# VectorE's sums of an eighth of a gate, issued one step behind their transfer

## The chip, the cores and the metric

The kernel runs on one core of a Trainium2 chip. The metric is the device time of one execution in microseconds (us), lower is better; of several runs the median counts. A profiled execution is one more run, with every instruction recorded.

## The reference, cut to what matters

One layer of a diffusion trunk is computed for two sets of 128 tokens, a prompt and a sample, which share all weights. All numbers are float32.

```python
mod = silu(cvec) @ w_ada + b_ada                  # 2048 x 12288: six pieces of 2048 columns
sh1, sc1, g1, sh2, sc2, g2 = split(mod, 6)
h = modulate(rmsnorm(x, norm_mix_w), sh1, sc1)
hq, hi, hff, hfb, hg, cb, cc, cx, nq, nk, nv = split(h @ w_in)
o = concat(hgrn2(hq, hi, hff, hfb, hg), short_conv(cb, cc, cx), attention(nq, nk, nv))
x = x + g1 * (o @ w_out)
h = modulate(rmsnorm(x, norm_ffn_w), sh2, sc2)
x = x + g2 * ((silu(h @ w_gate) * (h @ w_up)) @ w_down)
y = rmsnorm(x, final_norm_w)
```

The two gates g1 and g2 have 2048 columns each, in four chunks of 512. Each is a product of one row (the silu of the conditioning vector, a different one for prompt and sample) with 2048 x 512 weights.

## The kernel before, in words

**Stages.** First comes the modulation of the first norm and the input projections (w_in), then from about 235 us on the feature-major input projections (w_infm), between which the HGRN scan and the attention run, then the output projection (w_out, from about 526 us), the second norm (about 626 to 647 us), gate and up (w_gate, w_up) and the down projection (w_down) in two groups. Every weight tile of 128 x 2048 is loaded by SyncE's queue into one of four buffers `raw`, split by ScalarE into a rounded part `hi` and by VectorE into a remainder `lo` (line 254, or 295 for feature-major tiles), and multiplied three times by TensorE (lines 262 and 304).

**The later modulation.** The columns of w_ada that are needed later are computed beside these stages by two queues of steps. `LATER_T` goes to TensorE: `later_pe` loads a tile and issues four small products (`ada`, line 328), each into another 32 rows of one PSUM tile. `LATER_V` holds the seven gate chunks 8, 9, 10, 11, 21, 22 and 23 and goes to VectorE: `later_dve` handles an eighth of a chunk per step. A step takes one of two buffers `araw`, writes two of its columns by a GpSimd copy from the newest activations (line 407, so that the load can't start too early), issues a 512 KB load on GpSimd's queue (line 408), and adds the eighth to the accumulator `aacc` by four VectorE instructions (line 411), one for each of two rows of weights and two sets of tokens. With the first eighth the single accumulator is cleared and the bias loaded into it (lines 400 to 404); behind the last one `later_gate` is started, which broadcasts the sum over all partitions.

**What sets the order.** The main loops call `behind(phase)` after each weight tile; `ada_step` then adds the phase's pace to each queue's credit, and a step is run for each 4.0/n of credit, where n is the number of steps of a chunk. `gate(c)` runs what is left of a chunk when its gate is needed. What the program calls in this way is no final order: a list scheduler, which goes by the order of the calls as priorities, by data dependences, by free buffers and by its own simulated times, sets the order of each engine's instructions. On the chip each engine then works through its own list in that fixed order, and waits where the next instruction isn't ready.

Of the kernel before, what the change touches and what calls it, by code (L numbers as in the profile page):

```python
# [15 lines left out]
ALU = mybir.AluOpType  # L16
# [3 lines left out]
P = 128  # L20
D = 2048
CH = 512
# [8 lines left out]
LATER_T = [12, 16, 13, 17, 14, 18, 15, 19]  # L31
LATER_V = [8, 9, 10, 11, 21, 22, 23]
# [60 lines left out]
def trunk(ctx: ExitStack, tc: tile.TileContext, a: dict):  # L93
    nc = tc.nc
# [5 lines left out]
    def sb(shape, tag, bufs, dt=F32):  # L100
        uid[0] += 1
        return pool.tile(shape, dt, tag=tag, name=f"{tag}_{uid[0]}", bufs=bufs)

    def const(shape, name, dt=F32):
        return pool.tile(shape, dt, tag=name, name=name, bufs=1)
# [14 lines left out]
    def accs():  # L120
        r = []
        for s in range(2):
            uid[0] += 1
            r.append(psum.tile([P, CH], F32, tag="acc", name=f"acc_{uid[0]}", bufs=4))
        return r
# [25 lines left out]
    cs = const([P, 16, 2], "cs")  # L151
# [76 lines left out]
    def spawn(gen):  # L228
        if next(gen, active) is not active:
            active.append(gen)  # L230
# [129 lines left out]
    def later_gate(c, parts, pe):  # L360

        yield
        yield
        g = u4()
        hl = None
        for s in range(2):
            if hl is None or not pe:
                hl = [st(dt=F32R), st(dt=F32R)]
                nc.scalar.activation(hl[0], parts[s], AF.Copy)
                nc.vector.tensor_tensor(hl[1], parts[s], hl[0].bitcast(F32), op=ALU.subtract)  # L370
                yield
                yield
            ps = aux()
            for i in range(2):
                nc.tensor.matmul(ps, lhsT=selb[:, s, :] if pe else ones, rhs=hl[i], start=i == 0, stop=i == 1)  # L375
            nc.scalar.activation(g[:, s, :], ps, AF.Copy)
        gates[c] = g
# [18 lines left out]

    def later_dve(c, part, box):

        if part == 0:
            box["acc"] = sb([P, 2, CH], "aacc", 1)  # L400
            nc.gpsimd.tensor_copy(box["acc"][:, :, 0:1], S["late"][:, :, 0:1])  # L401
            nc.gpsimd.memset(box["acc"], 0.0)
            for s in range(2):
                nc.gpsimd.dma_start(box["acc"][0:1, s, :], a["b_ada"][0:1, c * CH:(c + 1) * CH])
        acc = box["acc"]
        raw = sb([P, 2, CH], "araw", 2)
        nc.gpsimd.tensor_copy(raw[:, :, 0:1], S["late"][:, :, 0:1])  # L407
        nc.gpsimd.dma_start(raw, a["w_ada2"][c - 8, part // 2, :, 2 * (part % 2):2 * (part % 2) + 2, :])  # L408
        for k in range(2):
            for s in range(2):  # L410
                nc.vector.scalar_tensor_tensor(acc[:, s, :], raw[:, k, :], cs[:, 2 * part + k, s:s + 1], acc[:, s, :],  # L411
                                               op0=ALU.mult, op1=ALU.add)
        if part == 7:
            spawn(later_gate(c, [acc[:, 0, :], acc[:, 1, :]], False))

    queues = []
    boxes = {}
    for chunks, fn, n in ((LATER_T, later_pe, 4), (LATER_V, later_dve, 8)):
        q = []
        for c in chunks:  # L420
            box = boxes.setdefault(c % 4 if c // 4 in (3, 4) else ("gate", c), {})
            q += [(fn, c, part, box) for part in range(n)]
        queues.append([q, 4.0 / n, 0.0])
# [64 lines left out]
    box = {}  # L488
# [40 lines left out]
    S = {}  # L529
# [333 lines left out]
    part = {}  # L863
    for ri, (k0, nk) in enumerate(ROUNDS):
# [4 lines left out]
        for i, name in enumerate(ORDER[:START]):  # L869
            acc = accs()  # L870
# [15 lines left out]
    for name in ORDER[START:]:  # L886
        if name in FM:
            for half in range(2):
                acc = accs()
# [7 lines left out]
        acc = accs()  # L897
# [11 lines left out]
    for n in range(4):  # L909
        acc = accs()  # L910
# [84 lines left out]
    for gi, grp in enumerate(groups):  # L995
# [6 lines left out]
        for n in range(4):  # L1002
            acc = accs()
# [113 lines left out]
```

## Time and profile before

| what | value |
|---|---|
| time, median of 3 runs | 1393.62 us (1393.14 to 1399.99) |
| profiled execution, own time | 1394.64 us |
| its span, first to last instruction | 1392.8 us |
| mean granted TensorE clock | 0.991 |
| TensorE busy | 1353.3 us, 97% of the span |
| VectorE busy | 875.9 us, 63% |
| sums of line 411 on VectorE | 224 instructions, 159.4 us |
| first and last start of line 411 | 219.8 us and 865.8 us |

The span is 1.8 us shorter than the run's own time. A product's record lasts longer than its share of the pipeline, so a busy TensorE doesn't mean that it is at its peak: its pace is read from the starts of products. Two passes over float32 operands stand as two records, so the four `ada` products of a tile are eight records. Buffer numbers are left out of names in the trace, and kept in the order shown below.

### The profile page before, as it was taken

How to read it: one execution, taken by the hardware profiler on the slowest of the kernel's cores; microseconds unless marked ns; L12 is line 12 of the kernel's file. 1: busy time of each engine (PE TensorE's matmuls, PEld its weight loads, DVE VectorE, ACT ScalarE, POOL GpSimd, SP SyncE). 2: the span in 40 equal slices, each digit the busy share in tenths (PEclk: the TensorE clock that was granted, in tenths of full speed). 3: DMA queues.
4: the chain of work that ended last, by engine and by line, in shares of the span. 5: the costliest groups of instructions: out<-in, count | busy, mean ns of one | idle time of the engine just before them, and what ended most of it. 6: DMA issues, size and time to landing. Idle time of an engine off the chain costs nothing.

```text
span 1392.8 us, 19779 instructions
## 1 busy us (share of the span) xinstructions
PE 1353.3 (97%) x7936; PEld 1082.0 (78%) x7936; DVE 875.9 (63%) x1102; ACT 626.6 (45%) x839; POOL 135.3 (10%) x201
## 2 busy tenths in 40 slices
PE   5999999999999999999899999999999999999996
PEld 3666777897798886677788788888888888888885
DVE  3354558987977886467745879545555544455565
ACT  4433347655455443346444344443334344444442
POOL 0100002221222321001200231000000000000000
PEclk9999999999999999999999999999999999999998
DMA  9797887775887988775665667555556555555551
GB/s 345 281 345 276 318 314 271 290 280 206 300 290 263 319 330 319 274 272 190 243 216 182 224 229 273 196 192 185 194 198 215 194 196 181 188 197 190 183 204 67
DMA packets 54380, 335.39 MB, mean 241 GB/s; under 512 B 7248, under 2 KB 7312, under 8 KB 19216
## 3 DMA queue, kind: packets, MB, share of 16 engines
q1 hardware_dynamic: 42768, 296.79, 58.7%
q0 software_dynamic: 10944, 36.29, 7.3%
q8 instruction: 62, 1.02, 0.3%
q10 hardware_dynamic: 576, 1.05, 0.2%
q14 instruction: 30, 0.25, 0.0%
HBM read 330.43 MB, written 3.67 MB: 240 GB/s over the span
## 4 chain that ended last, share of the span: by engine, by line
PE 89%; DMA 5%; issue 3%; DVE 2%; POOL 1%; ACT 1%; SPq 0%; DVEq 0%; POOLq 0%; ACTq 0%
PE acc L262 69%; PE acc L304 10%; PE ada L328 6%; DMA araw<-w_ada 2%; DMA raw<-w_ada 1%; PE aux L452 1%; DMA raw<-w_in 1%; DVE lo L254 1%; POOL araw L407 1%; DMA u<-xp 1%; PE aux L626 0%; PE aux L375 0%; DMA aacc<-b_ada 0%; DVE aacc L411 0%; PE aux L341 0%
## 5 line engine op out<-in xcount | busy, mean ns | idle before, releaser
L262 PE MATMUL acc<-hi,u 128*128 128x512 f32 x2944 | 873.4, 393 | 1.0 <-ACT u L484 0.8
L254 DVE TENSOR_TENSOR lo<-raw,hi 128x1024 fp32r<-128x1024 f32 x368 | 449.2, 1223 | 376.2 <-ACT hi L253 362.3
L262 PEld LDWEIGHTS acc<-hi,u 128*128 128x128 f32 x2944 | 551.6, 189 | 136.8 <-issue 11.2
L253 ACT ACTIVATE hi<-raw 128x1024 fp32r<-128x1024 f32 x368 | 388.7, 1060 | 556.1 <-PE acc L262 471.8
L262 PE MATMUL acc<-lo,u 128*128 128x512 f32 x1472 | 533.1, 394 | 7.1 <-DVE lo L254 7.1
L262 PEld LDWEIGHTS acc<-lo,u 128*128 128x128 f32 x1472 | 274.5, 188 | 77.5 <-DVE lo L254 11.6
L411 DVE SCALAR_TENSOR_TENSOR aacc<-araw,cs,aacc 128x512 f32<-128x512 f32 x224 | 159.4, 746 | 40.7 <-DMA araw<-w_ada 31.1
L304 PE MATMUL acc<-u,hi 128*128 128x256 f32 x768 | 141.8, 286 | 0.0
L304 PEld LDWEIGHTS acc<-u,hi 128*128 128x128 f32 x768 | 119.0, 191 | 7.3 <-issue 5.9
L304 PE MATMUL acc<-u,lo 128*128 128x256 f32 x384 | 108.1, 286 | 0.0
L328 PE MATMUL ada<-raw,cst 128*32 128x256 f32 (+1 forms) x784 | 92.3, 481 | 11.8 <-DMA raw<-w_ada 11.8
L407 POOL COPY araw<-u 128x2 f32<-128x2 f32 x56 | 54.0, 965 | 264.4 <-DVE aacc L411 212.7
L294 ACT ACTIVATE hi<-raw 128x1024 fp32r<-128x1024 f32 x48 | 50.9, 1060 | 64.0 <-PE acc L304 44.0
L304 PEld LDWEIGHTS acc<-u,lo 128*128 128x128 f32 x384 | 72.5, 191 | 5.2 <-issue 2.5
L295 DVE TENSOR_TENSOR lo<-raw,hi 128x1024 fp32r<-128x1024 f32 x48 | 58.4, 1221 | 15.3 <-ACT hi L294 12.5
L328 PEld LDWEIGHTS ada<-raw,cst 128*32 128x32 f32 x784 | 26.4, 113 | 44.3 <-issue 32.1
L878 DVE TENSOR_TENSOR u<-u,acc 128x512 f32<-128x512 f32 x56 | 37.7, 684 | 26.7 <-PE acc L262 26.7
L408 POOL DMA_DIRECT2D araw<-w_ada x56 | 30.0, 536 | 15.5 <-POOL araw L407 15.2
L401 POOL COPY aacc<-u 128x2 f32<-128x2 f32 x7 | 3.8, 536 | 252.3 <-DVE u L878 173.4
L480 ACT ACTIVATE st<-aux,sh,sc 128x128 f32<-128x128 f32 x48 | 18.1, 456 | 14.3 <-DVE sc L349 7.4
L262 PE MATMUL acc<-u,u 128*128 128x512 f32 x96 | 22.1, 389 | 0.0
L262 PEld LDWEIGHTS acc<-u,u 128*128 128x128 f32 x96 | 18.0, 188 | 3.7
(218 smaller groups left out, 631.8 us busy)
## 6 DMA issues: line engine op xcount, KB each, us to landing
raw<-w_ada SPq DMA_DIRECT2D x66, 1024.0 KB, 6.9
raw<-w_gate SPq DMA_DIRECT2D x44, 1024.0 KB, 4.9
raw<-w_up SPq DMA_DIRECT2D x44, 1024.0 KB, 4.8
raw<-w_down SPq DMA_DIRECT2D x44, 1024.0 KB, 4.8
raw<-w_in SPq DMA_DIRECT2D x33, 1024.0 KB, 6.5
araw<-w_ada POOLq DMA_DIRECT2D x56, 512.0 KB, 5.7
raw<-w_infm SPq DMA_DIRECT2D x24, 1024.0 KB, 6.2
raw<-w_out SPq DMA_DIRECT2D x16, 1024.0 KB, 5.8
```

The source lines that it names most:

```text
L253: nc.scalar.activation(hi, raw[:, 2 * j:2 * j + 2], AF.Copy)
L254: nc.vector.tensor_tensor(lo, raw[:, 2 * j:2 * j + 2], hi.bitcast(F32), op=ALU.subtract)
L262: nc.tensor.matmul(acc, lhsT=lhs[:, s, x, lk, :], rhs=w[:, k % 2, :], start=first and i == 0, stop=last and i == 2)
L294: nc.scalar.activation(hi, raw[:, 4 * j:4 * j + 4], AF.Copy)
L295: nc.vector.tensor_tensor(lo, raw[:, 4 * j:4 * j + 4], hi.bitcast(F32), op=ALU.subtract)
L304: nc.tensor.matmul(one, lhsT=w[:, k % 4, ws], rhs=y, start=first and k == 0 and i == 0, stop=last and k == 7 and i == 2)
L328: nc.tensor.matmul(box["acc"][32 * k:32 * k + 32, 0:cols.stop - cols.start], lhsT=cst[:, 4 * part + k, 2 - row:34 - row], rhs=raw[k // 2][ ...
L407: nc.gpsimd.tensor_copy(raw[:, :, 0:1], S["late"][:, :, 0:1])
L408: nc.gpsimd.dma_start(raw, a["w_ada2"][c - 8, part // 2, :, 2 * (part % 2):2 * (part % 2) + 2, :])
L411: nc.vector.scalar_tensor_tensor(acc[:, s, :], raw[:, k, :], cs[:, 2 * part + k, s:s + 1], acc[:, s, :], op0=ALU.mult, op1=ALU.add)
L480: nc.scalar.activation(h[:, s, j, :], ps[:, s, j, :], AF.Identity, bias=bias, scale=scale)
L878: nc.vector.tensor_tensor(part[name][:, s, :], part[name][:, s, :], acc[s], op=ALU.add)
```

## The change

Of each step of `later_dve` the four sums now belong to the eighth before: step 0 loads the first eighth, steps 1 to 7 load one and add the one before, step 8 adds the last one and starts `later_gate`. A chunk so has 9 steps in place of 8, and the credit that each costs is 4.0/9 in place of 4.0/8. The instructions are the same in kind and number.

```diff
-        raw = sb([P, 2, CH], "araw", 2)
-        nc.gpsimd.tensor_copy(raw[:, :, 0:1], S["late"][:, :, 0:1])
-        nc.gpsimd.dma_start(raw, a["w_ada2"][c - 8, part // 2, :, 2 * (part % 2):2 * (part % 2) + 2, :])
-        for k in range(2):
-            for s in range(2):
-                nc.vector.scalar_tensor_tensor(acc[:, s, :], raw[:, k, :], cs[:, 2 * part + k, s:s + 1], acc[:, s, :],
-                                               op0=ALU.mult, op1=ALU.add)
-        if part == 7:
+        if part < 8:
+            raw = sb([P, 2, CH], "araw", 2)
+            nc.gpsimd.tensor_copy(raw[:, :, 0:1], S["late"][:, :, 0:1])
+            nc.gpsimd.dma_start(raw, a["w_ada2"][c - 8, part // 2, :, 2 * (part % 2):2 * (part % 2) + 2, :])
+            box[part] = raw
+        if part > 0:
+            for k in range(2):
+                for s in range(2):
+                    nc.vector.scalar_tensor_tensor(acc[:, s, :], box[part - 1][:, k, :], cs[:, 2 * (part - 1) + k, s:s + 1],
+                                                   acc[:, s, :], op0=ALU.mult, op1=ALU.add)
+        if part == 8:
             spawn(later_gate(c, [acc[:, 0, :], acc[:, 1, :]], False))
...
-    for chunks, fn, n in ((LATER_T, later_pe, 4), (LATER_V, later_dve, 8)):
+    for chunks, fn, n in ((LATER_T, later_pe, 4), (LATER_V, later_dve, 9)):
```

Line numbers behind the change are higher by up to five: line 411 becomes 416, line 452 becomes 457.

TensorE, at the first feature-major tile (248 us in the trace of before). `acc` are the sums of the main products, `ada` is the sum of the small ones, `raw` their weights. Before:

```order
L304 MATMUL acc_1961<-u_105_580,hi_1969 128x256 x2
L304 MATMUL acc_1962<-u_105_580,hi_1969 128x256 x2
L328 MATMUL ada_1575<-raw_2192,cst 32x512 x4
L304 MATMUL acc_1961<-u_105_580,lo_1970 128x256
L304 MATMUL acc_1962<-u_105_580,lo_1970 128x256
```

and now:

```order
L631 MATMUL aux_1904<-u_319_1773,u_332_1864 32x32 x6
L304 MATMUL acc_1957<-u_22_189,hi_1961 128x256 x2
L328 MATMUL ada_1575<-raw_2188,cst 32x512
L304 MATMUL acc_1958<-u_22_189,hi_1961 128x256 x2
L328 MATMUL ada_1575<-raw_2188,cst 32x512 x3
L304 MATMUL acc_1957<-u_22_189,lo_1962 128x256
```

The four small products of one weight tile stood together and are now one and three, with two main products between them; they also stand earlier, at the tile's first `hi` in place of its second.

TensorE, in the attention stage (430 us in the trace of before); `aux` of line 762 (now 767) are scores. Before:

```order
L304 MATMUL acc_4203<-u_105_580,lo_4211 128x256
L762 MATMUL aux_4183<-st_3804,u_572_3824 128x128 x4
L328 MATMUL ada_4072<-raw_4282,cst 32x512 x4
L304 MATMUL acc_4202<-u_167_921,hi_4297 128x256 x2
L304 MATMUL acc_4202<-u_167_921,lo_4298 128x256
```

and now:

```order
L304 MATMUL acc_4206<-u_105_580,lo_4214 128x256
L328 MATMUL ada_4068<-raw_4285,cst 32x512 x2
L767 MATMUL aux_4179<-st_3807,u_572_3824 128x128 x4
L328 MATMUL ada_4068<-raw_4285,cst 32x512 x2
L304 MATMUL acc_4205<-u_167_921,hi_4300 128x256 x2
```

Here too four that stood together now stand as two and two.

VectorE, in the gate and up projections (677 to 687 us in the trace of before). Before:

```order
L411 SCALAR_TENSOR_TENSOR aacc_5805<-araw_6619,cs,aacc_5805 128x512
L411 SCALAR_TENSOR_TENSOR aacc_5805<-araw_6713,cs,aacc_5805 128x512
L254 TENSOR_TENSOR lo_6301<-raw_6294,hi_6300 128x1024
L411 SCALAR_TENSOR_TENSOR aacc_5805<-araw_6713,cs,aacc_5805 128x512 x3
L254 TENSOR_TENSOR lo_6336<-raw_6333,hi_6335 128x1024
```

and now:

```order
L416 SCALAR_TENSOR_TENSOR aacc_5796<-araw_6581,cs,aacc_5796 128x512
L416 SCALAR_TENSOR_TENSOR aacc_5796<-araw_6656,cs,aacc_5796 128x512
L254 TENSOR_TENSOR lo_6297<-raw_6290,hi_6296 128x1024
L416 SCALAR_TENSOR_TENSOR aacc_5796<-araw_6656,cs,aacc_5796 128x512 x3
L254 TENSOR_TENSOR lo_6332<-raw_6329,hi_6331 128x1024
```

Nothing has moved here: only the numbers of the buffers differ.

## Rows read from the trace of the kernel before

**Rows 1.** The page's busy times: us, share of the span, instructions.

```profile
PE 1353.3 (97%) x7936; PEld 1082.0 (78%) x7936; DVE 875.9 (63%) x1102; ACT 626.6 (45%) x839; POOL 135.3 (10%) x201
```

**Rows 2.** Waits of PE, 220 to 600 us: total us, times, longest.

```profile
PE ada L328 <- DMA raw<-w_ada: 0.7, 1, 0.7
PE aux L682 <- issue: 0.4, 1, 0.4
```

**Rows 3.** Waits of PE, 600 to 870 us.

```profile
PE acc L262 <- DVE lo L254: 7.1, 6, 2.3
```

**Rows 4.** Waits of DVE for the gate's loads, 220 to 600 us.

```profile
DVE aacc L411 <- DMA araw<-w_ada: 11.5, 9, 3.9
DVE aacc L411 <- DMA aacc<-b_ada: 3.5, 4, 2.1
```

**Rows 5.** Waits of DVE for the gate's loads, 600 to 870 us.

```profile
DVE aacc L411 <- DMA araw<-w_ada: 19.5, 9, 3.6
DVE aacc L411 <- DMA aacc<-b_ada: 5.9, 3, 2.4
```

**Rows 6.** Timeline of DVE, one such wait: start us, us, instruction, [idle before].

```profile
678.87 0.74 DVE L411 SCALAR_TENSOR_TENSOR aacc<-araw,cs,aacc 128x512 f32<-128x512 f32 x1
683.20 0.75 DVE L411 SCALAR_TENSOR_TENSOR aacc<-araw,cs,aacc 128x512 f32<-128x512 f32 x1 [3.59 <-DMA araw<-w_ada]
683.87 1.22 DVE L254 TENSOR_TENSOR lo<-raw,hi 128x1024 fp32r<-128x1024 f32 x1
```

**Rows 7.** Timeline of POOL, the load that this wait is for.

```profile
674.75 1.78 POOL L407 COPY araw<-u 128x2 f32<-128x2 f32 x1 [6.36 <-DVE aacc L411]
676.83 0.53 POOL L408 DMA_DIRECT2D araw<-w_ada  x1 [0.30 <-POOL araw L407]
```

**Rows 8.** Timeline of PE at the same place.

```profile
681.73 1.07 PE L262 MATMUL acc<-hi,u 128*128 128x512 f32 x4
685.15 1.22 PE L262 MATMUL acc<-lo,u 128*128 128x512 f32 x2 [2.35 <-DVE lo L254]
```

**Rows 9.** Stretches: PE, PEld, DVE, ACT, POOL busy (instructions), granted clock, DMA, GB/s.

```profile
685.20:688.40 3.20, 3.20 (x8) 2.55 (x9) 3.20 (x5) 0.00 (x0) 1.12 (x1) 0.50 0.70 212
797.00:801.00 4.00, 4.00 (x11) 3.17 (x12) 4.00 (x6) 1.06 (x1) 0.93 (x1) 0.59 0.71 252
```

**Rows 10.** Timeline of PE, four small products together.

```profile
247.50 0.64 PE L304 MATMUL acc<-u,hi 128*128 128x256 f32 x4
248.07 1.07 PE L328 MATMUL ada<-raw,cst 128*32 128x512 f32 x8
249.06 0.50 PE L304 MATMUL acc<-u,lo 128*128 128x256 f32 x2
```

**Rows 11.** Timeline of PE, one small product alone.

```profile
315.57 0.84 PE L262 MATMUL acc<-hi,u 128*128 128x512 f32 x3
316.34 1.04 PE L328 MATMUL ada<-raw,cst 128*32 128x512 f32 x2
317.32 0.73 PE L262 MATMUL acc<-lo,u 128*128 128x512 f32 x2
317.88 0.39 PE L262 MATMUL acc<-hi,u 128*128 128x512 f32 x1
```

**Rows 12.** Chain that ended last, an undisturbed stretch: start us, us, what.

```profile
926.05 174.10 PE acc L262 x768
```

**Rows 13.** Timeline of PE, 64-column products split, then together.

```profile
295.45 0.33 PE L649 MATMUL aux<-u,u 128*64 128x64 f32 x2
295.71 0.50 PE L304 MATMUL acc<-u,hi 128*128 128x256 f32 x2
...
296.26 1.15 PE L649 MATMUL aux<-u,u 128*64 128x64 f32 x30
297.33 0.50 PE L304 MATMUL acc<-u,hi 128*128 128x256 f32 x2
...
386.62 1.15 PE L649 MATMUL aux<-u,u 128*64 128x64 f32 x32
387.71 0.55 PE L452 MATMUL aux<-ident,u 128*128 128x128 f32 x3
```

**Rows 14.** Timeline of SyncE, the load of an `ada` tile.

```profile
379.02 0.33 SPq L324 DMA_DIRECT2D raw<-w_ada  x1
```

**Rows 15.** Timeline of PE, the small products of the tile before that one.

```profile
383.76 1.07 PE L328 MATMUL ada<-raw,cst 128*32 128x512 f32 x8
```

**Rows 16.** Loads into `raw`, 225 to 600 us, from issue to landing.

```profile
DMA to landing us min/median/max: 4.6/6.1/9.8
```

**Rows 17.** Timeline of DVE, ahead of SyncE's load.

```profile
376.45 1.41 DVE L411 SCALAR_TENSOR_TENSOR aacc<-araw,cs,aacc 128x512 f32<-128x512 f32 x2
377.78 1.22 DVE L295 TENSOR_TENSOR lo<-raw,hi 128x1024 fp32r<-128x1024 f32 x1
```

## The prediction

> **What bounds the kernel now.** I read the page's busy times first: TensorE is busy for 97% of the span, VectorE for 63% [rows 1]. TensorE sets the end, so an edit on VectorE or GpSimd counts only as far as it makes TensorE wait or gives it other work. Next I read the waits of TensorE, cut at the two parts of the stretch in which the changed steps run. From 220 to 600 us it waits 1.1 us in all, and for no sum [rows 2]. From 600 to 870 us it waits six times for a `lo` of VectorE, 7.1 us together, 2.35 us at the longest [rows 3, 8]. Then the waits of VectorE for the gate's loads: 15.0 us in the first part, 25.4 us in the second [rows 4, 5]. So in the first part these waits are covered: TensorE has other tiles ready. In the second part they are not. One of the six shows the chain: GpSimd's copy waits until a buffer `araw` is free, its load is issued at 676.83 us, VectorE sits 3.59 us before the sum that needs it, the `lo` queued behind that sum starts at 683.87 us, and TensorE stands until 685.15 us [rows 6 to 8]. That is what the edited line orders could touch.
>
> Such a wait costs more than itself. After the 2.35 us TensorE's granted clock was 0.50 for 3.2 us, which is the 1.2 GHz level; a second such stretch has 0.59 over 4 us [rows 9]. At half the pace these lose 1.6 us each (3.20 x 0.50, and 4.00 x 0.41).
>
> **The change part by part.** *The sums and loads themselves.* As many as before, of the same kind: nothing added, nothing removed. *The program's order from 536 us on.* Here the lists of all five engines are the same as before, instruction for instruction and buffer for buffer: VectorE's last 530 rows of 998, TensorE's last 2,418 of 4,099, ScalarE's last 416 of 702, GpSimd's last 73 of 193, and all of SyncE's 299 in kind. The scheduler had put each sum where its own clock saw the load landed, and a lower priority of sums that are anyway the last to become ready moves none of them. The sums still stand between the same two `lo`s as before, so the six waits stay: gain 0. If they went, 7.1 + 2 x 1.6 = 10.3 us would.
>
> *The order between 225 and 536 us.* Here it moves. The second load goes ahead of the scan state's loads on GpSimd, some sums move past a `lo` or two, and ScalarE and TensorE follow. VectorE has idle time there, and TensorE's cover held under waits of up to 3.9 us [rows 4], so moved sums alone cost nothing; if that cover is gone, a wait like the ones of the second part would show, up to 2.35 us each [rows 8]. What does cost is how the small products `ada` are cut up, since they are TensorE's own time. The four of a weight tile go to four different quarters of the array and run beside one another: all four take 249.06 - 248.07 = 0.99 us [rows 10], and one alone takes 317.32 - 316.34 = 0.98 us [rows 11]. A main product takes 174.10/768 = 0.227 us [rows 12]. Around the lone one the three products before it take 316.34 - 315.57 = 0.77 us in place of 0.68, the two behind it 317.88 - 317.32 = 0.56 in place of 0.45. So one more group costs 0.98 + 0.09 + 0.11 = 1.18 us, whatever it holds from one to four. I counted passes (a group of up to four is one, of five to eight two) in both orders of TensorE's list:
>
> - tile loaded as raw_2192 before: 1 group, now 2 (the first place shown)
> - raw_3026: one and three before, now one, one and two: 2 becomes 3
> - raw_4282: 1 becomes 2 (the second place shown)
> - raw_4402 with raw_4449: six and two, 3 passes, now five, one and two: 4
> - raw_4530: one and three before, now four together: 2 becomes 1
>
> All others keep their number. Net three passes more: 3 x 1.18 = +3.54 us.
>
> Around them: groups that now stand directly beside a group of 32-column products of the scan save an entry and an exit, 0.20 us each; there are four such places now and two before, -0.40. Two tiles stand together as eight, which saves one more, -0.20. A group of sixteen 64-column products is now cut into one and fifteen. Cut as it stood elsewhere it takes 0.26 + 1.07 us, together 1.09 [rows 13], plus 0.20 for the entry and exit: +0.44. Sum of the three -0.16 us.
>
> The Trainium skill, TensorEngine Tiling (Array Packing), section Tiling Modes, speaks against this change: a change of tiling mode drains TensorE. By that alone three more groups would cost their entries and exits, 3 x 0.20 = 0.6 us, and the kernel would be at no change. The same section's rule that tiles run independently agrees with one pass for one or four, and the row of the lone product, 0.98 us, decides for the larger price.
>
> *Waits that the new order of the first part adds or takes away.* The trace can't show them. Below: all of TensorE's old waits there go, -1.1 us [rows 2]. Above: a late load stops TensorE, worked out below as +5.7 us. I take 0: with a much similar order this stretch of 300 us had 1.1 us in all, and that is the nearest row.
>
> Sum: 3.54 - 0.16 + 0 = +3.4 us. Against the profiled execution's own 1394.64 us (span 1392.8 and 1.8 around it) that is 1398.0. This execution lies 1.0 us above the median of 1393.62 us, so the median of the changed kernel comes to 1397.0 us, 0.24% slower than before. A measurement of this kernel can tell about 0.5%, 7 us, from no change, so this counts as no change.
>
> **The rivals.**
>
> *The waits of 600 to 870 us go.* That would be sums that no longer sit in VectorE's list ahead of their landing: 1393.6 + 3.4 - 10.3 = 1386.7 us, or 1383.3 without the added passes. For it speaks that the waits are real and on TensorE's path [rows 3, 6 to 8]. Against it speaks the order: same rows, same two buffers, same loads behind the same releases. Only a shift of GpSimd's loads against TensorE by several us could do it, and both hang on the same tiles. Chance 0.05.
>
> *The change does nothing to the time.* The lists shift, but later waits take up what the added passes cost: a TensorE that comes 3.4 us later finds a `lo` ready for which it waited, if VectorE's chain doesn't shift with it. The 7.1 us of waits [rows 3] would be enough. Against it: VectorE's `lo`s wait for buffers that TensorE frees, so the chain moves with it. Time 1393.6 us, chance 0.15.
>
> *Slower: a load lands behind the two tiles that now stand together.* At 383.76 us in the trace of before TensorE ran four small products [rows 15]; the next tile's four, which stood well behind main products before, now stand directly behind them, so they want their tile at 384.8 us. Its load was issued at 379.02 us [rows 14], which leaves 5.8 us; the median from issue to landing is 6.1 us and the longest 9.8 us [rows 16]. At 9.8 us TensorE stands 4.0 us, everything of its list behind it, and loses some 1.6 us more at the lower clock [rows 9]: +5.7 us, 1393.6 + 3.4 + 5.7 = 1402.7 us. Against it: the `lo` that frees this load's buffer now stands two sums earlier on VectorE, 377.78 - 376.45 = 1.3 us [rows 17], and the added passes bring TensorE there 2.4 us later, so it decides from a landing of about 9.5 us on. A wait of like size at another moved place would look the same. Chance 0.15.
>
> **How the numbers follow.** The sum has 0.65, and the rivals 0.05, 0.15 and 0.15. Predicted: 1397.0 us. Its own range, from the lower bound of the added waits to a few small ones, is 1395 to 1400. The range for 8 in 10 takes in the case of no effect and most of the late load, and about 1 us of run to run: 1392 to 1402.5. Faster by over 0.5% (under 1386.7) is the first rival, 0.05. Slower by over 0.5% (over 1400.6) is the late load, and a little of the sum with several small waits: 0.17. The rest, 0.78, is within 0.5%.
>
> **What would show it.** TensorE's waits for `lo` between 600 and 870 us, shifted by some us, again six and about 7 us. The four sums of each eighth at 660 to 690 us between the same `lo`s, with a wait of VectorE of some 3.6 us ahead of one of them. Lone small products near 248, 316 and 430 us with about 1 us each until the next main product. No new wait of TensorE above 1 us before 536 us; the place to look is right behind 384 us. The prediction is wrong if TensorE's waits behind 600 us have changed by more than 2 us with this same order, or if lone groups of small products cost less than 0.9 us.

## The result and the profile after

The changed kernel takes 1401.25 us (median of 20 executions, 1398.50 to 1408.25), the kernel before 1393.80 us (20 executions beside it, 1392.42 to 1399.99). The ratio is 1.0052 (95% interval 1.0041 to 1.0063), which is 7.2 us slower. That is inside the predicted range of 1392 to 1402.5 us, 4 us above the predicted time, and just in the class "slower by over 0.5%", which the prediction gave 0.17. The profiled execution of the changed kernel took 1398.5 us (span 1396.7), its fastest.

The page's busy times after (us, share, instructions), against [rows 1]:

```profile
PE 1355.4 (97%) x7936; PEld 1081.8 (77%) x7936; DVE 876.0 (63%) x1102; ACT 626.5 (45%) x839; POOL 134.4 (10%) x201
```

The groups by line show where TensorE's 2 us come from. The small products `ada` in the kernel before, and then after (instructions | busy us, mean ns | idle before them):

```profile
L328 PE MATMUL ada<-raw,cst 128*32 128x256 f32 (+1 forms) x784 | 92.3, 481 | 11.8 <-DMA raw<-w_ada 11.8
```

```profile
L328 PE MATMUL ada<-raw,cst 128*32 128x256 f32 (+1 forms) x784 | 95.1, 479 | 11.9 <-DMA raw<-w_ada 11.9
```

The same 784 records take 2.8 us more, as three more passes should. One of the cut groups, PE's timeline after (start us, us, instruction):

```profile
245.67 1.04 PE L328 MATMUL ada<-raw,cst 128*32 128x512 f32 x2
246.64 0.50 PE L304 MATMUL acc<-u,hi 128*128 128x256 f32 x2
247.08 1.06 PE L328 MATMUL ada<-raw,cst 128*32 128x512 f32 x6
248.06 0.50 PE L304 MATMUL acc<-u,lo 128*128 128x256 f32 x2
```

A product alone keeps TensorE 0.97 us, the other three together 0.98 us (246.64 - 245.67, 248.06 - 247.08). In [rows 10] the four together took 0.99.

TensorE's waits after, 220 to 605 us, and then 605 to 880 us, against [rows 2, 3]:

```profile
PE aux L457 <- DMA ld<-ck: 1.4, 1, 1.4
PE acc L262 <- DVE lo L254: 1.2, 1, 1.2
PE acc L304 <- DVE lo L295: 0.7, 1, 0.7
```

```profile
PE acc L262 <- DVE lo L254: 6.8, 6, 2.4
PE aux L474 <- DVE st L487: 0.9, 1, 0.9
```

In this trace the same six waits stand behind 605 us. The one followed in [rows 6 to 8] is there again, 5 us later and link by link: POOL's copy and load, VectorE's sum and `lo`, TensorE.

```profile
679.76 1.78 POOL L410 COPY araw<-u 128x2 f32<-128x2 f32 x1 [6.48 <-DVE aacc L416]
681.84 0.53 POOL L411 DMA_DIRECT2D araw<-w_ada  x1 [0.30 <-POOL araw L410]
...
688.22 0.75 DVE L416 SCALAR_TENSOR_TENSOR aacc<-araw,cs,aacc 128x512 f32<-128x512 f32 x1 [3.60 <-DMA araw<-w_ada]
688.89 1.22 DVE L254 TENSOR_TENSOR lo<-raw,hi 128x1024 fp32r<-128x1024 f32 x1
...
690.16 0.73 PE L262 MATMUL acc<-lo,u 128*128 128x512 f32 x2 [2.35 <-DVE lo L254]
```

In front of 605 us, 3.3 us of waits stand where 1.1 stood, two of them over 1 us. VectorE's waits for gate loads in that part grew from 11.5 to 20.4 us [rows 4]:

```profile
DVE aacc L416 <- DMA araw<-w_ada: 20.4, 11, 4.1
DVE aacc L416 <- DMA aacc<-b_ada: 2.5, 2, 2.1
```

To size it, I timed the stretch between two instructions that stand ahead of and behind everything that moved: the last transposes before the scan and the first product of the output gate's `ada`. PE's timeline, before and then after:

```profile
215.42 0.60 PE L452 MATMUL aux<-ident,u 128*128 128x128 f32 x4
...
612.22 1.05 PE L328 MATMUL ada<-u,cst 128*32 128x512 f32 x4
```

```profile
214.85 0.60 PE L457 MATMUL aux<-ident,u 128*128 128x128 f32 x4
...
617.35 1.05 PE L328 MATMUL ada<-u,cst 128*32 128x512 f32 x4
```

That is 396.80 us before and 402.50 us after, +5.7. What follows is 780.6 and 779.3 us.

### The profile page after: what moved, and what is told of

Same layout as the page of the kernel before. It is cut to its first block, busy times and chain, and to the rows that moved or that the text cites. A ratio compares the mean times of both kernels' runs of the same rounds, so it can differ in the third digit from the quotient of the medians.

```text
span 1396.7 us, 19774 instructions
## 1 busy us (share of the span) xinstructions
PE 1355.4 (97%) x7936; PEld 1081.8 (77%) x7936; DVE 876.0 (63%) x1102; ACT 626.5 (45%) x839; POOL 134.4 (10%) x201
## 4 chain that ended last, share of the span: by engine, by line
PE 80%; DMA 8%; issue 5%; DVE 3%; POOL 2%; ACT 1%; SPq 0%; DVEq 0%; POOLq 0%; ACTq 0%
PE acc L262 65%; PE acc L304 7%; PE ada L328 5%; DMA araw<-w_ada 5%; DVE aacc L416 1%; DMA raw<-w_ada 1%; POOL araw L410 1%; DMA raw<-w_in 1%; DVE lo L254 1%; PE aux L457 1%; DMA ld<-ck 1%; DMA u<-xp 1%; ACT hi L253 0%; PE aux L631 0%; DMA aacc<-b_ada 0%
## 5 line engine op out<-in xcount | busy, mean ns | idle before, releaser
L328 PE MATMUL ada<-raw,cst 128*32 128x256 f32 (+1 forms) x784 | 95.1, 479 | 11.9 <-DMA raw<-w_ada 11.9
L328 PEld LDWEIGHTS ada<-raw,cst 128*32 128x32 f32 x784 | 26.7, 112 | 45.0 <-issue 32.9
```

Of the source, the lines that this page charges most:

```text
L328: nc.tensor.matmul(box["acc"][32 * k:32 * k + 32, 0:cols.stop - cols.start], lhsT=cst[:, 4 * part + k, 2 - row:34 - row], rhs=raw[k // 2][ ...
```

## The experiments

**Three more traces of the changed kernel, and what varies.** The kernel is unchanged; the first expectation:

> The changed kernel again, unchanged, for a second trace. Its times run from 1398.5 to 1408.3 us, those of the kernel before mostly from 1392.4 to 1395.4, and the first trace of it (1398.5 us) is its fastest execution. Theory A: the waits that the new order adds in 225 to 536 us vary from run to run, above all the one for the load of ck and cv at 404 us (1.4 us in the first trace) and the half clock that may follow it. Then a trace of a slower execution shows that wait, or another PE wait before 536 us, larger by about as much as the execution is slower. Rival B: the waits for a lo of 600 to 870 us vary (6.8 us in the first trace, 7.1 us in the kernel before). Then the first part repeats with 2.2 us of new waits and the second part is longer.

It took 1397.1 us, less than any execution so far, and so it could not show what a slower one has. The `ck` wait was 0.2 us, the `lo` at 241 us came in time, and the `lo` at 521 us cost 2.0 us. Two more:

> The changed kernel once more, for a third trace. The first two (1398.5 and 1397.1 us) have waits of TensorE of 3.3 and 2.2 us between 220 and 605 us, in different places but one. Theory A: between the first common instruction ahead of the changed stretch and the first one behind it, the time without TensorE's stalls of over 0.5 us is the same in every execution, 3 to 4 us above the kernel before (370.8 and 371.6 us against 367.4), and what an execution is slower beyond that is stalls at some of four places: the lo at 241 us, the loads near 264 to 275 us, the load of ck at 403 us, the lo at 523 us. Rival B: the stretch outside (ahead of 182 us or behind 552 us) carries what varies.

> As the look before: the stretch from 182 to about 555 us holds the difference to the kernel before (5 to 10 us, of it 3 to 4 us outside stalls), and the rest of the span is within 1.5 us of the kernel before.

They took 1401.4 and 1401.2 us, both near the median. In both, what lies outside the stretch of the table is within 1.5 us of the kernel before. The table takes the stretch between the two instructions above for each trace that has them in this form: its length, TensorE's waits of over 0.3 us in it, what it lost where the granted clock was under 0.97 (length x (1 - clock), in slices of 4 us), what is left (waits of under 0.3 us are still in it), and the span behind it. Each row is one execution: that of the delay alone is the fastest of its ten, those of the last two rows are the second slowest of their sets.

| trace | stretch | waits | clock | left | behind |
|---|---|---|---|---|---|
| before, 1394.6 us | 396.8 | 1.6 | 0 | 395.2 | 780.6 |
| delay alone, 1392.2 us | 396.8 | 1.8 | 0 | 395.0 | 778.6 |
| changed, 1397.1 us | 400.9 | 2.0 | 0 | 399.0 | 780.5 |
| changed, 1398.5 us | 402.5 | 3.6 | 0 | 398.9 | 779.3 |
| changed, 1401.2 us | 402.5 | 3.8 | 0 | 398.7 | 782.0 |
| changed, 1401.4 us | 402.6 | 2.6 | 1.7 | 398.3 | 782.1 |
| ninth step alone, 1401.8 us | 403.4 | 4.4 | 0 | 399.0 | 782.0 |
| `ck`, `cv` on SyncE, 1402.5 us | 408.2 | 7.6 | 1.6 | 399.0 | 778.6 |

The column "left" is nearly the same in all of the nine-step orders, 398.3 to 399.0, and 3.1 to 4.0 us above the two of the old order. That agrees with the work term, +3.4 in the prediction. The rest varies: waits at a handful of places, and the clock after them. Theory A had this right for the stretch, but not alone. Behind the stretch the kernels vary by 3.5 us, with no difference that plainly goes with the order; the two executions near the median had 1.4 us more there than the kernel before had in its profile. So rival B has a part of what makes an execution slow. Most of that part, too, is waits and the clock after them: taken out in the same way, up to 12 us before the end, they leave 770.0 to 771.0 us in all eight traces. The wait that differs most is the one for a `lo` near 814 us: 0.2 us in the kernel before (810 us there) and 0.4 us in the first trace after, but 1.8 to 1.9 us in the other three traces of the changed kernel.

The most frequent of the new waits is the `lo` at about 521 us. First the kernel before, VectorE's timeline there:

```profile
513.38 1.23 DVE L295 TENSOR_TENSOR lo<-raw,hi 128x1024 fp32r<-128x1024 f32 x1 [0.59 <-ACT hi L294]
...
516.25 1.23 DVE L254 TENSOR_TENSOR lo<-raw,hi 128x1024 fp32r<-128x1024 f32 x1
518.78 1.41 DVE L411 SCALAR_TENSOR_TENSOR aacc<-araw,cs,aacc 128x512 f32<-128x512 f32 x2 [1.30 <-DMA araw<-w_ada]
```

And the changed kernel, execution of 1401.4 us, timeline of VectorE and then TensorE:

```profile
520.91 1.42 DVE L416 SCALAR_TENSOR_TENSOR aacc<-araw,cs,aacc 128x512 f32<-128x512 f32 x2 [5.29 <-DMA araw<-w_ada]
522.25 1.22 DVE L295 TENSOR_TENSOR lo<-raw,hi 128x1024 fp32r<-128x1024 f32 x1
...
520.99 0.40 PE L304 MATMUL acc<-u,hi 128*128 128x256 f32 x2
523.52 0.39 PE L304 MATMUL acc<-u,lo 128*128 128x256 f32 x1 [2.13 <-DVE lo L295]
```

The 4 us behind that wait in the same trace (busy times of PE, PEld, DVE, ACT and POOL, then granted clock, DMA, GB/s):

```profile
524.00:528.00 4.00, 4.00 (x25) 3.63 (x27) 3.78 (x8) 0.45 (x1) 2.85 (x2) 0.58 0.79 280
```

Before, the sum that sat for its load stood behind the last `lo` of line 295 and one of the next matrix. Now it stands ahead of the last of line 295, which TensorE is already asking for: 2.13 us, and for most of the next 4 us the clock was at its lower level (4.00 x 0.42 = 1.7 us lost). In the executions of 1397.1 and 1401.2 us the same `lo` came 1.97 and 2.24 us late and the clock stayed at 1.00, so the same wait costs 2 or nearly 4 us.

**The delay alone.** Same eight steps; an eighth's sums are issued with the next step, the last two eighths with the last:

```
+        box[part] = raw
+        for p in ((part - 1, part) if part == 7 else (part - 1,) if part else ()):
             for k in range(2):
...
```

> Sums one step behind their load as in the changed kernel, but in eight steps: the last step adds the last two eighths. Theory A: the order of instructions on all five engines is that of the kernel before, so the delay by itself changes nothing: 1393.8 us within 0.1%. Rival B, by which issuing the sums later costs the 7 us, gives 1400 us or more.

Measured 1393.94 us, ratio 0.9992 (0.9978 to 1.0005). Its only wait of TensorE from 220 to 605 us:

```profile
PE ada L328 <- DMA raw<-w_ada: 1.5, 1, 1.5
```

All five engines keep the order of before, and no change of the time shows. The edit that gives the change its name does nothing by itself that these runs can tell.

**The ninth step alone.** `n` is 9, each eighth's sums stay in its own step, and the ninth only starts the gate:

```
+        if part < 8:
...
+        if part == 8:
             spawn(later_gate(c, [acc[:, 0, :], acc[:, 1, :]], False))
...
-    for chunks, fn, n in ((LATER_T, later_pe, 4), (LATER_V, later_dve, 8)):
+    for chunks, fn, n in ((LATER_T, later_pe, 4), (LATER_V, later_dve, 9)):
```

> The gate's steps are nine in place of eight and their credit per weight tile is that of the changed kernel, but each eighth's sums stay in the step that loads it; the ninth step only starts the gate. Theory A: the ninth step, not the delay of the sums, moves the order: TensorE's small products take 49 passes as in the changed kernel (46 before), so 3 x 1.18 = 3.5 us more, and GpSimd issues the loads of ck and cv equally late. Expected about 1400 to 1402 us, the changed kernel's own time. Rival B: the sums that are issued one step behind cost the time. Then this kernel runs at 1393.8 us, as before, or at least under 1396.

Measured 1398.79 us, ratio 1.0026 (1.0015 to 1.0037): 3.6 us over the kernel before, which ran at 1395.16 us beside it. The `ada` products take what they take in the changed kernel:

```profile
L328 PE MATMUL ada<-raw,cst 128*32 128x256 f32 (+1 forms) x784 | 95.4, 480 | 12.6 <-DMA raw<-w_ada 12.6
```

So the ninth step, which makes the credit of a step 4/9 in place of 4/8, brings the three passes, and half of the change's 7.2 us. It is 1.2 us faster than I expected, and its interval doesn't overlap with that of the changed kernel, though the two were not timed beside each other. Given nine steps the delay moves some more of the order. One such place is the `lo` at 521 us: in this kernel's trace the sums ahead of it waited 1.08 us for their load and TensorE didn't wait there, while all four traces of the changed kernel have that wait, 0.7 to 2.2 us. With one trace of this kernel, whether that is the whole of the other half stays open.

**The loads of `ck` and `cv` on SyncE.** In the changed kernel GpSimd issues them late (`ck` at 394.31 us, against 386.17 in the kernel before) and TensorE waits. GpSimd's timeline there, and TensorE's:

```profile
388.18 2.33 POOL L410 COPY araw<-u 128x2 f32<-128x2 f32 x1 [5.42 <-DVE aacc L416]
...
394.31 0.82 POOL L734 DMA_DIRECT2D ld<-ck  x1
...
404.39 0.63 PE L457 MATMUL aux<-ident,ld 128*128 128x128 f32 x4 [1.39 <-DMA ld<-ck]
```

```
-        nc.gpsimd.dma_start(kv[:, 0, :], a["ck"])
-        nc.gpsimd.dma_start(kv[:, 1, :], a["cv"])
+        nc.sync.dma_start(kv[:, 0, :], a["ck"])
+        nc.sync.dma_start(kv[:, 1, :], a["cv"])
```

> The changed kernel with one edit: the loads of ck and cv are issued on SyncE instead of GpSimd, so they no longer stand in GpSimd's queue behind the copy into araw at 388 us. TensorE, VectorE and ScalarE keep their order. Theory A: the wait of TensorE for ck at 404 us (1.4 us in the first trace, more in slower executions) and what follows it is the part that the sum of the prediction left out: the median falls from 1401.3 to about 1397 to 1398 us, the times lie closer together, and the wait is gone from the trace. Rival B: the extra is elsewhere, in the order itself: the median stays at 1400 to 1402 us.

Measured 1400.13 us (1393.84 to 1406.54), ratio 1.0037 (1.0020 to 1.0053). The wait is gone and the times did not close up, so the part of theory A that said why the times vary falls. The median stands 5.0 us over the kernel before beside it, where the changed kernel's stood 7.2; these intervals overlap, so a gain of some 2 us is neither shown nor excluded. This execution (1402.5 us) had four late `lo` instead:

```profile
PE acc L304 <- DVE lo L295: 6.2, 4, 2.3
PE ada L328 <- DMA raw<-w_ada: 1.0, 1, 1.0
```

The first of the four, on GpSimd and VectorE:

```profile
249.12 6.39 POOL L410 COPY araw<-u 128x2 f32<-128x2 f32 x2 [23.94 <-DVE u L883]
255.45 1.07 POOL L411 DMA_DIRECT2D araw<-w_ada  x2
...
253.11 2.36 DVE L295 TENSOR_TENSOR lo<-raw,hi 128x1024 fp32r<-128x1024 f32 x2
255.38 0.45 DVE L633 COPY_PREDICATED st<-lvl,aux 128x256 f32<-128x256 uint8 x1
263.43 1.42 DVE L416 SCALAR_TENSOR_TENSOR aacc<-araw,cs,aacc 128x512 f32<-128x512 f32 x2 [6.23 <-DMA araw<-w_ada]
```

In the changed order two copies of GpSimd stand together here with both loads behind them. They ended at 255.51 us, just after VectorE's run of two-input operations, so both loads went out 3.7 us later than in the first trace after (251.74 us), and the sum sat 6.23 us ahead of a `lo`. In the first trace after, the same two copies took:

```profile
251.23 0.31 POOL L410 COPY araw<-u 128x2 f32<-128x2 f32 x2 [23.17 <-DVE u L883]
```

In both traces they started some 0.15 us after the same VectorE operation (line 633), so 6 us of copy came or didn't come at a place that the edit doesn't touch. No single queue explains these traces: the moved order waits at several places, and at which of them differs between executions.

**Without GpSimd's two-column copies.** From the third eighth of a gate on, the copy ahead of the load is left out, in the changed kernel and in the kernel before; the sum that frees the buffer then holds the load itself.

```
-            nc.gpsimd.tensor_copy(raw[:, :, 0:1], S["late"][:, :, 0:1])
+            if part < 2:
+                nc.gpsimd.tensor_copy(raw[:, :, 0:1], S["late"][:, :, 0:1])
```

> The changed kernel without GpSimd's two-column copy ahead of each gate load, from the third eighth of a gate on (the first two keep it, the sums are the same, and the buffer's release now holds the load itself). The order moves again; TensorE's list has 46 passes, as the kernel before. Theory A: the new waits for a lo come from sums of VectorE that stand ahead of it and sit for a load that is issued late; without the copies (0.2 to 6.4 us each in the traces, and 0.3 us to the issue) the loads land earlier, VectorE's waits for araw shrink from 40 us to under 30, and TensorE's waits for lo after 600 us from 7 us to 4 or less: 1389 to 1393 us. Rival B: the copies cost nothing that TensorE sees, since the release by the sum sets the load: the waits after 600 us stay at 7 us and the time at that of the kernel before, 1394 us, or above it by waits at new places.

> The kernel before with the same edit (no two-column copy of GpSimd ahead of the gate loads from the third eighth on): 47 passes in place of 46, eight steps. Theory A: loads that are issued earlier shrink the waits for lo after 600 us from 7 us to 4 or less, against 1.2 us for the added pass: 1389 to 1393 us. Rival B: no change, 1394 to 1396 us, the six waits stay.

Measured: the changed kernel 1381.73 us, ratio 0.9920 (0.9908 to 0.9932); the kernel before 1384.60 us, 0.9943 (0.9930 to 0.9957). Both went further than theory A, whose conditions hold: in the changed kernel VectorE's waits for `araw` fell from 40.0 to 20.3 us. In that kernel without copies, GpSimd's timeline at one load:

```profile
672.43 0.53 POOL L412 DMA_DIRECT2D araw<-w_ada  x1 [5.52 <-DVE aacc L417]
```

TensorE's waits there from 600 to 870 us:

```profile
PE acc L262 <- DVE lo L254: 1.0, 1, 1.0
PE aux L475 <- DVE st L488: 0.9, 1, 0.9
```

The load goes out at the sum's end; in [rows 7] copy and hand-over took 2.1 us (676.83 - 674.75). Of six late `lo` one is left, and no slice of 180 to 880 us has the lower clock. The prediction's first rival put the prize of these waits at 10.3 us; here nearly all of them went, with a gain of 11.2 us against the 1392.94 of the kernel before beside it. The order moved as well, so the copies' own share isn't separated from that.

**The four products of a tile kept together.** A high priority on the four `ada` products:

```
-        for k in range(4):
+        with tc.high_priority(offset=1500):
+            for k in range(4):
...
```

> The kernel before with one edit: the four small products ada of a weight tile get a high priority, so the scheduler keeps them together. TensorE's list has 38 passes of 512-column ada products in place of 46; the delay and the ninth step are not in it. Theory A: a pass costs 1.18 us, whether it holds one product or four (rows 10 and 11), so eight passes fewer give 8 x 1.18 = 9.4 us, about 0.7% under the kernel before. Rival B: only the entry and exit of a group cost, 0.2 us each: 1.6 us less, not to be told from no change. Rival C: kept together they stand closer to their weight tile's landing and TensorE waits there: what the passes save is lost in waits for raw, no change or slower.

> The changed kernel with the same edit (the four small products of a weight tile kept together): 38 passes as well, 11 fewer than the changed kernel has. Theory A: with equal passes the rest of the change's cost shows by itself, the waits that the moved order adds: 11 x 1.18 = 13 us under the changed kernel, and 0 to 4 us above the kernel before with this edit. Rival B: the passes are no part of the change's cost, and the difference of 5 to 7 us between the changed kernel and the kernel before is there between these two as well.

Measured 1388.54 us, ratio 0.9963 (0.9949 to 0.9978), and 1388.60 us, 0.9956 (0.9935 to 0.9977). With the passes made equal by this edit, no difference shows between the two orders, within some 3 us either way. The second is 12.7 us under the changed kernel, as theory A had it. In the kernel before with this edit, the group of the products:

```profile
L329 PE MATMUL ada<-raw,cst 128*32 128x256 f32 (+1 forms) x784 | 76.1, 488 | 19.5 <-DVE r_t L206 9.9 <-DMA raw<-w_ada 9.6
```

Its waits of TensorE from 220 to 560 us:

```profile
PE acc L304 <- DVE lo L295: 8.6, 4, 3.6
PE ada L329 <- DMA raw<-w_ada: 2.9, 1, 2.9
PE acc L304 <- ACT hi L294: 0.6, 1, 0.6
```

These products take 16.2 us less; those of the tiles loaded as `u`, which are not in this row, take 1.2 us more (4.2 for 3.0). I had expected 9.4, counting only the 512-column products. They give about 7 us of busy time, and the 256-column ones ahead of 225 us, which I had not counted and which were cut up too, another 8. Some 11 us of it came back as waits, 12.1 us where 1.1 stood [rows 2]: theory A in kind, with about half of the price from products that it left out, and rival C in that waits took most of it back, though more for `lo` than for `raw`.

**Both edits.** Offset 400 here, with the same 38 passes:

> The changed kernel with both edits: no two-column copy of GpSimd ahead of the gate loads from the third eighth on, and the four small products of a weight tile kept together (38 passes in place of 46 without this edit). Theory A: the two gains add up, 8 x 1.18 = 9.4 us less than the 1381.7 us without the copies, less the few us of waits for raw and lo that keeping the products together cost: 1374 to 1379 us. Rival B: with the products kept together TensorE stands for its weight tiles and the passes saved come back as waits: 1381 us or more.

> The kernel before with both edits (no copies from the third eighth on, the four products together, 38 passes in place of 47). Theory A: 1384.6 us less 9 x 1.18 = 10.6 us, plus a few us of waits: 1375 to 1380 us. Rival B: the passes saved come back as waits: 1384 us or more.

Measured 1379.11 us for the changed kernel, ratio 0.9893 (0.9876 to 0.9909): little more of a gain than without the copies alone, at the upper edge of theory A's range. For the kernel before, 1367.82 us, 0.9810 (0.9792 to 0.9827): 26.7 us faster than the kernel before beside it, 7 better than theory A's best, and the fastest of all. All its waits of TensorE from 220 to 870 us:

```profile
PE aux L471 <- DVE u L955: 3.2, 1, 3.2
PE aux L471 <- DVE st L484: 0.9, 1, 0.9
PE ada L329 <- DMA raw<-w_ada: 0.2, 1, 0.2
```

No `lo` is late. In this kernel, with the copies gone, the passes saved stay saved. In the changed kernel they don't. It has the same 38 passes and is 11.3 us slower, and from 220 to 560 us TensorE waits 8.0 us where 0.2 stand above, most of it here:

```profile
PE ada L329 <- DMA raw<-w_ada: 4.4, 4, 2.0
PE aux L633 <- DVE u L611: 2.1, 1, 2.1
```

So the passes are not all that separates the two orders. Against the kernel of eight steps, that of nine is 7.2 us slower as the two stand, no different with the products kept together, about 3 us faster without the copies (ratios 0.9920 and 0.9943, intervals that just meet), and 11.3 us slower with both edits. Why one order meets these waits and another doesn't is not shown.

## Why the prediction was right, and where it fell short

*The range, partly by luck.* The result lies inside 1392 to 1402.5 us, but outside the sum's own range of 1395 to 1400. The upper end came from a tile for `ada` that lands late, which didn't happen; waits at other places filled it.

*Sums and loads, 0.* Right: the delay alone is at 0.9992.

*The six waits behind 536 us stay.* Right in the first trace: six again, 6.8 us against 7.1, the shown one 2.35 us in both. Equal lists kept these waits, but not their sizes: the other three traces have 7.7 to 8.8 us, and that of the ninth step alone, with the same list there, 10.3. The first rival's gain came with the edit that leaves out the copies, not with the delay.

*Three passes, +3.54, and -0.16 around them.* Right in kind and size: +2.8 us busy, and 3.1 to 4.0 us of stretch without waits and clock. The Trainium skill, TensorEngine Tiling (Array Packing), Tiling Modes, says that a change of tiling mode drains TensorE. Entries and exits alone, 0.20 us a group by [rows 11, 12], would have been 0.6 us for three groups; that is the small part of the 3.1 to 4.0 us.

*New waits, taken as 0 with bounds -1.1 and +5.7.* This step failed, by its size: it is the term of the sum that was mis-sized. The four traces of the changed kernel have 0.4 to 2.2 us more waits in the stretch, and one has 1.7 us of lower clock besides; the stretch as a whole is 4.1 to 5.8 us longer. The sign "no new wait of TensorE above 1 us before 536 us" failed in each of them. "This stretch had 1.1 us in all with a similar order" was the wrong row to go by: sums there sat up to 3.9 us, and the list of VectorE showed a sum moving ahead of the `lo` that TensorE asks for next. The row to take was that wait of 2.35 us of the second part, with a chance at each place where a waiting sum moves ahead of a `lo`. The sum also left out that GpSimd's loads of `ck` and `cv` would be issued behind a copy for a gate load.

*No effect, since later waits absorb it.* Wrong: what follows the stretch did not get shorter by what the stretch got longer.

*Slower by a late load.* A late load did stop TensorE, but a gate's load by way of VectorE, at another place: no small product waited right behind 384 us. The price, +5.7 us, also doesn't follow from the prediction's own rows: it says that the load decides from a landing of about 9.5 us on, and then a landing at 9.8 us stops TensorE for 0.3 us, not 4.0. A load that lands late plus the lower clock is what the `lo` at 521 us paid in one of four traces, 2.13 + 1.7 us.

*The median.* Against before's profile, the two executions near 1401.3 us have +5.7 and +5.8 us in the stretch, +1.4 and +1.5 behind it, and -0.5 ahead. The part behind has 1.1 and 2.2 us more of waits over 0.3 us in these two (its six waits for a `lo` were 7.7 and 8.8 us), and in the second 1.6 us less is lost to the clock. Why just these executions met longer waits there is not shown.

## What to carry to other kernels

Where a scheduler sets the order, compare the lists before arguing from the edit's intent: here the delay by itself moved nothing, and a step count that only set a credit moved the order over 300 us. When an in-order engine's waiting instruction moves ahead of one that feeds the bottleneck, price that wait even if it was covered before. And look at what stands between a buffer's release and the load that refills it: in the kernel before, keeping the small products together gained 0.4% with the two-column copies there, and 1.3% without them.

## What the runs showed of the hardware

GpSimd's copy of two columns takes from 0.18 to 4.9 us in the kernel before, and up to 6.3 us in the trace with `ck` and `cv` on SyncE. In the kernel before, GpSimd's copy and VectorE's operations beside it:

```profile
252.12 4.86 POOL L407 COPY araw<-u 128x2 f32<-128x2 f32 x1 [1.37 <-DVE aacc L411]
...
254.58 2.35 DVE L295 TENSOR_TENSOR lo<-raw,hi 128x1024 fp32r<-128x1024 f32 x2
256.85 0.44 DVE L628 COPY_PREDICATED st<-lvl,aux 128x256 f32<-128x256 uint8 x1
```

It ended at 256.98 us, 0.13 us after VectorE went from its operations with two inputs to one of another kind; in the trace with `ck` and `cv` on SyncE it was 0.13 us as well (255.51 against 255.38). The Trainium skill, SBUF — State Buffer, SBUF: two separate sides, says that VectorE's operations with two SBUF inputs and a GpSimd operation that reads SBUF exclude each other by a lock. Both places agree with that; no run here isolates it.

A stall of about 2 us was followed by the lower clock in some executions and not in others, at the same instruction: 0.58 over 4 us behind 2.13 us, and 1.00 behind 1.97 and 2.24 us. Such a stretch cost 1.6 us in [rows 9] and 1.7 us here.
